# A linear map after a pooling folded into the projection before it, in a two-layer streaming encoder

## The chip, the core and the metric

The kernel runs on one core of a Trainium2 chip. A core has five engines that run side by side, each with its own instruction stream in a fixed order: TensorE (PE: matrix products and transposes; its weight loads are shown apart as PEld), VectorE (DVE), ScalarE (ACT), GpSimd (POOL) and SyncE (SP, which here only issues transfers). They work on an on-chip memory of 128 partitions; TensorE writes to a second one, PSUM, from which DVE and ACT read. The weights, the inputs and most intermediate results lie in DRAM. The metric is the device time of one execution in microseconds (us); lower is better.

## The reference

Two layers over one sequence of 2048 tokens with 1024 channels. Only layer 0's mixer matters here:

```python
def pool_mixer(h, w_in, w_group, scale, w_out):
    u, z = jnp.split(h @ w_in, 2, axis=-1)
    u = u.reshape(B, S, N_POOL_GROUPS, POOL_GROUP_DIM)      # 4 groups of 256 channels
    cs = jnp.cumsum(u, axis=1)
    ...
    for g, w in enumerate(POOL_WINDOWS):                    # 2, 4, 8, 16 frames
        ...
        means.append((cs[:, :, g] - lo) / cnt)
    pooled = jnp.stack(means, axis=2) - u
    mixed = jnp.einsum('bsgc,gcd->bsgd', pooled, w_group).reshape(B, S, D_MODEL) * scale
    return (mixed * jax.nn.silu(z)) @ w_out
```

`h` is the input after an RMS norm. For each group of channels the trailing mean over its window, minus the frame itself, is taken along the tokens; a 256 x 256 map then mixes the channels of the group. The pooling works along tokens only, with the same numbers for every channel of a group, and the map along channels only, so the two may be exchanged. After the mixer come a residual, a gated per-layer embedding, one key and value projection, and layer 1 with causal stick-breaking attention over 16 heads, a gate, an output projection and a second gated embedding.

## The kernel before

**Tiling.** The tokens are worked off in four chunks of 512 (`s`). Products run at float32 accuracy from pairs: a value is split into a high part and the rest, both in a format that TensorE reads at full rate, and each product is three matmuls (high x high, high x low, low x high) of 128 x 128 weights with 512 columns. `product` (L119) does this for two output tiles at a time over eight k-tiles: 48 matmuls. `split` (L168) makes a pair from a source: ACT casts the high part, DVE or POOL subtracts to get the low one.

**The steps of a chunk.** `steps` (L475) lists, for each chunk, 22 steps with a loader and a function that runs it. For the groups 3, 2, 1, 0 in turn there is a u step (`run_u`, L218) and a z step (`run_z`, L253); then come four output-projection steps (`run_o`, L281), four embedding steps (`run_g`, L309) and six query, key and value steps (`run_kvq`, L345). The main loop (L532) calls the loader of the next step before it runs the present one. I call a product by its step: u3 is the product of group 3's u, z2 that of group 2's z.

**The mixer.** `run_u` makes u of a group (48 matmuls), scales it by the token's norm (`ub`, L230; `rb` is that norm, broadcast), and pools it: the windowed sum is built by doubling (`us`, L236; the first and last additions on DVE, the middle ones on POOL), then `po` is the mean minus the frame (L240). In chunk 0 the first frames are corrected (L244, L245). `po` is split into the pair `pp` (L246). `run_z` makes z and SiLU(z) (L260 to L262, left in `zs`). `run_m` (L268) multiplies `pp` by the group's map (12 matmuls, the weights from `a_w_group`), then by scale and SiLU(z) (`mf`, L275), and splits the result into the pair `mp`, which `run_o` reads. `run_o` takes the k-tiles of groups 3, 2, 1, 0 in this order. `run_m` of a group stands behind the u product of the next group.

**Weights.** `load_w` (L85) loads raw weights from DRAM into the pool `wraw` (three buffers) and splits them into the pool `wpair` (twelve buffers), the input projection's with the norm's gain multiplied in (ACT at L107, DVE at L108). The split input-projection weights are stored to DRAM (`wi`, L112), and chunks 1 to 3 load them from there (L96), with no conversion. Loads and stores are issued in one queue, SP's; an issue that waits holds up those behind it. The pool `io` (ten buffers) holds the inputs and other raw tiles, `act` (18 buffers) the pairs.

**Kept weights.** `keep` (L499) loads a piece of layer 1's weights, splits it and stores it for the attention stage. The main loop calls one or two of these a step from step 8 of a chunk on.

**What sets the order.** The program's text gives a priority, and a scheduler then orders each engine's instructions ahead of time, so that a load or a split may stand well ahead of its place in the text; `tc.keep_in_program_order` takes an instruction out of this. Buffers come from pools: a new tile takes one that is free, or waits for the last reader of one. PSUM has six buffers for products (`dense`) and two for transposes (`turned`).

**Layer 1** runs in a second part (from L545 on) and is not touched. Its attention does, among others, matmuls of 128 x 128 weights with 128 to 512 columns on the diagonal blocks (L598, L599) and transposes (L623).

Of the kernel before, what the change touches and what calls it, by code (L numbers as in the profile page):

```python
# [34 lines left out]
def trunk_kernel(ctx, tc, x, p, a_norm, a_w_in, a_w_group, a_scale, a_w_out, kv_norm, w_kv,  # L35
# [46 lines left out]
    state = {"w": 0, "first": True}  # L82
    split_once = {}

    def load_w(pools, src, kts, c0, n, gain=None, kept=None):  # L85
# [6 lines left out]
        for k0 in range(0, kts, kk):  # L92
# [5 lines left out]
            raw = wraw.tile([P, kk, n], F32, tag="wraw", name="wraw")  # L98
# [20 lines left out]
    def product(pss_, units, acts, c0s, order=None):  # L119

        order = order or range(len(acts))
        for kt in order:
            for ps, c0 in zip(pss_, c0s):
                T.matmul(ps, wst(units, kt, 0, c0), acts[kt][:, 0], start=(kt == order[0]), stop=False)  # L124
                T.matmul(ps, wst(units, kt, 0, c0), acts[kt][:, 1], start=False, stop=False)  # L125
                T.matmul(ps, wst(units, kt, 1, c0), acts[kt][:, 0], start=False, stop=(kt == order[-1]))  # L126

# [7 lines left out]
    with ExitStack() as st:  # L135
# [36 lines left out]
        chunk = [{"zs": {}, "pooled": {}, "m": {}} for _ in range(NSUB)]  # L172
# [45 lines left out]
        def run_u(s, g, wu, wg=None):  # L218
            ck, win = chunk[s], WIN[g]
            pss2 = [dense(), dense()]  # L220
            product(pss2, wu, ck["x"], (0, P))
# [3 lines left out]
            pooled = []  # L225
            for k in range(2):
# [19 lines left out]
                pp = pair("pp")  # L246
                split(pp, po, V)
                pooled.append(pp)
            ck["pooled"][g] = pooled
            if wg is not None:  # L250
                run_m(s, g + 1, wg)

        def run_z(s, g, wz, wg=None):  # L253
            ck = chunk[s]
            pss2 = [dense(), dense()]
            product(pss2, wz, ck["x"], (0, P))
            zs = []
            for k in range(2):
                zr, sg = tmp("zr"), tmp("sg")
                V.tensor_tensor(out=zr, in0=pss2[k], in1=ck["rb"], op=ALU.mult)  # L260
                A.activation(out=sg, in_=zr, func=AF.Sigmoid)
                G.tensor_tensor(out=zr, in0=zr, in1=sg, op=ALU.mult)  # L262
                zs.append(zr)
            ck["zs"][g] = zs
            if wg is not None:
                run_m(s, g, wg)

        def run_m(s, g, wg):  # L268
            ck = chunk[s]
            pss2 = [dense(), dense()]  # L270
            product(pss2, wg, ck["pooled"].pop(g), (0, P))
            for k in range(2):
                o = 2 * g + k
                mf = tmp("mf")
# [599 lines left out]
```

## Time and profile before

| | |
|---|---|
| Median of 3 runs | 2869.15 us (2866.77 to 2869.49) |
| The profiled execution: its time | 2867.54 us |
| its span in the profile | 2865.7 us |
| Chunk 0: first input product to first output product | 15.02 to 132.54 us |
| Chunk 1: the same | 383.89 to 482.30 us |
| Attention's first matmul | 1416.2 us |
| DMA over the span | 576 MB, 201 GB/s |

The page of the profile gives each engine's busy time and share of the span. Its groups of instructions show the line, engine, operation, output <- input, shape and count, then busy time and mean duration, then how long the engine was idle just before them and what ended that. A timeline row gives start, duration, engine, line, operation and tiles; the bracket at its end is the idle time before it and what released it. Matmuls overlap in the pipeline, so the distance between two starts, not the duration, is what one occupies. DMA shares are means over 16 DMA engines.

### The profile page before, as it was taken

To read this page: it belongs to the slowest core of one execution; us is meant where nothing else is said; L and a number is where in the kernel's file an instruction comes from. 1 tells how busy PE (TensorE), PEld (TensorE's weight loads), DVE (VectorE), ACT (ScalarE), POOL (GpSimd) and SP (SyncE) were. 2 spreads that over 40 slices of the span, in tenths; PEclk is the share of its full clock that TensorE was granted. 3 is DMA by queue.
4 is the path that set the end of the run, shared out by engine and by line. 5 is a ranking of instruction groups with operands and counts; after the bars stand their busy time and mean duration, and the time that the engine had idled before them with its cause. 6 is when DMAs were issued, how large, how long until landed. Compare 5 with 4: busy or idle time off the path is not lost. (4 is left out here: it accounts for less than half of the span.)

```text
span 2865.7 us, 40527 instructions
## 1 busy us (share of the span) xinstructions
PE 2763.3 (96%) x13667; PEld 2273.2 (79%) x13667; DVE 1893.8 (66%) x2581; ACT 1405.6 (49%) x2765; POOL 956.2 (33%) x965
## 2 busy tenths in 40 slices
PE   8899999999999999999899999999999999999999
PEld 6688788888888888888777888787877778878877
DVE  5645535455355543555299989999999988886642
ACT  4444523355234542345255555656566655554431
POOL 3464347542474425743212121221111122213220
PEclk9999999999999999999999999999999999999999
DMA  7756696467955678446657565555555556667765
GB/s 265 257 162 216 220 305 208 143 205 250 306 160 169 223 243 287 136 153 207 212 188 229 163 216 170 159 164 177 165 161 161 163 176 193 186 188 243 251 207 158
DMA packets 335139, 576.43 MB, mean 201 GB/s; under 512 B 32782, under 2 KB 161838, under 8 KB 334932
## 3 DMA queue, kind: packets, MB, share of 16 engines
q1 hardware_dynamic: 327944, 564.34, 61.2%
q10 hardware_dynamic: 6988, 9.50, 1.1%
q8 instruction: 108, 1.77, 0.3%
q14 instruction: 99, 0.81, 0.1%
HBM read 433.16 MB, written 132.19 MB: 197 GB/s over the span
## 5 line engine op out<-in xcount | busy, mean ns | idle before, releaser
L353 PE MATMUL psd<-wpair,x 128*128 128x512 f32 x2304 | 544.8, 393 | 0.0
L602 ACT ACTIVATE kap<-psl 128x512 f32<-128x512 f32 (+3 forms) x640 | 340.3, 533 | 407.6 <-PE psl L599 398.3
L609 DVE TENSOR_TENSOR_SCAN pp<-kap,pp,zeros 128x512 f32<-128x512 f32 x384 | 512.2, 1338 | 23.3 <-ACT kap L602 21.2
L353 PEld LDWEIGHTS psd<-wpair,x 128*128 128x128 f32 x2304 | 428.8, 188 | 86.4
L623 PE MATMUL psa<-ident,pp 128*128 128x128 f32 x2176 | 348.7, 275 | 42.7 <-DVE at L627 37.9
L627 DVE TENSOR_TENSOR at<-psa,at 128x512 fp32r<-128x512 f32 (+3 forms) x640 | 373.5, 586 | 14.8 <-ACT at L626 13.8
L623 PEld LDWEIGHTS psa<-ident,pp 128*128 128x128 f32 x2176 | 263.5, 141 | 127.0 <-DVE at L627 71.2
L626 ACT CAST at<-psa 128x512 fp32r<-128x512 f32 (+3 forms) x640 | 331.3, 519 | 51.7 <-PE psa L623 48.5
L604 POOL TENSOR_SCALAR_AFFINE_SELECT kap<-kap 128x128 f32<-128x128 f32 x256 | 88.0, 345 | 633.1 <-ACT kap L602 597.9
L609 DVE TENSOR_TENSOR_SCAN pp<-kap,zeros 128x128 f32<-128x128 f32 (+3 forms) x256 | 214.2, 838 | 93.7 <-POOL kap L604 92.4
L598 PE MATMUL psl<-kk,qa 128*128 128x512 f32 (+3 forms) x640 | 235.0, 367 | 7.0 <-ACT vr L390 5.2
L635 PE MATMUL pso<-at,vv 128*128 128x512 f32 (+3 forms) x640 | 235.2, 367 | 0.8 <-ACT at L626 0.7
L599 PE MATMUL psl<-kk,qb 128*128 128x512 f32 (+3 forms) x640 | 235.1, 367 | 0.0
L636 PE MATMUL pso<-at,vv 128*128 128x512 f32 (+3 forms) x640 | 234.1, 366 | 0.0
L126 PE MATMUL psd<-xp,wpair 128*128 128x512 f32 x512 | 201.2, 393 | 4.3 <-DVE wpair L108 4.2
L124 PE MATMUL psd<-xp,wpair 128*128 128x512 f32 x512 | 201.0, 393 | 3.6 <-ACT xp L169 2.4
L108 DVE SCALAR_TENSOR_TENSOR wpair<-wraw,gains,wpair 128x512 fp32r<-128x512 f32 x192 | 149.5, 790 | 82.1 <-ACT wpair L107 81.8
L125 PE MATMUL psd<-xp,wpair 128*128 128x512 f32 x512 | 200.7, 392 | 0.0
L107 ACT ACTIVATE wpair<-wraw,gains 128x512 fp32r<-128x512 f32 x192 | 136.8, 720 | 121.0 <-DMA wraw<-in_w_kv_dram 65.9
L103 POOL TENSOR_TENSOR wpair<-wraw,wpair 128x512 fp32r<-128x512 f32 x107 | 147.7, 1388 | 78.5 <-ACT wpair L101 58.8
L101 ACT CAST wpair<-wraw 128x512 fp32r<-128x512 f32 x160 | 96.1, 619 | 124.1 <-DMA wraw<-in_a_w_out_dram 51.5
L598 PEld LDWEIGHTS psl<-kk,qa 128*128 128x128 f32 x640 | 120.9, 189 | 28.7 <-ACT vr L390 5.7
(204 smaller groups left out, 5553.4 us busy)
## 6 DMA issues: line engine op xcount, KB each, us to landing
wpair<-wi SPq DMA_DIRECT2D x96, 512.0 KB
kk<-kd SPq DMA_DIRECT2D x320, 128.0 KB
vv<-vd SPq DMA_DIRECT2D x160, 256.0 KB
wraw<-in_w_kv_dram SPq DMA_DIRECT2D x128, 256.0 KB
wpair<-wzd SPq DMA_DIRECT2D x64, 512.0 KB
wpair<-wod SPq DMA_DIRECT2D x64, 512.0 KB
wpair<-wgd SPq DMA_DIRECT2D x64, 512.0 KB
wi<-wpair SPq DMA_DIRECT2D x32, 512.0 KB
```

Of the source, the lines that this page charges most:

```text
L124: T.matmul(ps, wst(units, kt, 0, c0), acts[kt][:, 0], start=(kt == order[0]), stop=False)
L126: T.matmul(ps, wst(units, kt, 1, c0), acts[kt][:, 0], start=False, stop=(kt == order[-1]))
L353: T.matmul(pss2[i], ck["x2"][kt][:, xh, tk], wst(ws, kt, wh, 0, W5), start=(kt == 0 and xh == 0 and wh == 0), stop=(kt == KT - 1 and wh == 1))
L598: T.matmul(ps[:, :w], qa[:, qs], kk[:, :w], start=True, stop=False)
L599: T.matmul(ps[:, :w], qb[:, qs], kk[:, :w], start=False, stop=True)
L602: A.activation(out=kp[:, r0:], in_=ps[:, :w], func=AF.Sigmoid, scale=-1.0)
L609: V.tensor_tensor_scan(out=pp[:, r0:][:, ::-1], data0=kp[:, r0:][:, ::-1], data1=zeros.to_broadcast([P, w]), initial=1.0 if st["diag"] els ...
L623: T.transpose(pt[:, j * P : (j + 1) * P], pp[:, r0 + kt * P : r0 + (kt + 1) * P], ident)
L626: A.copy(out=at[:, 0, cs], in_=pt[:, cs])
L627: V.tensor_tensor(out=at[:, 1, cs], in0=pt[:, cs], in1=f(at[:, 0, cs]), op=ALU.subtract)
L635: T.matmul(po[:, cs], vv[:, kt, :], at[:, 0, cs], start=(st["diag"] and kt == 0), stop=False)
L636: T.matmul(po[:, cs], vv[:, kt, :], at[:, 1, cs], start=False, stop=(st["last"] and kt == 3))
```

## The change

The group map goes from the pooled activations to the weights. In chunk 0, for each group, the weights of u (1024 x 256) are multiplied by the group's 256 x 256 map once, with the norm's gain, on TensorE; the product is split into a pair and stored as the input-projection weight. u made with it is already mapped, so that `run_m` is gone in all chunks, and `po` is multiplied by scale and SiLU(z) at once and split into `mp`.

- z now comes ahead of u in each group, since u's step needs SiLU(z).
- `load_fold` loads a group's raw u weights (into pairs of the pool `act`) and its map. `fold` transposes the raw weights in blocks of 128 x 128 (`across`: 16 transposes and four splits into `wt` for a group), then multiplies (`mapped`: four times 12 matmuls with 256 columns), and evicts with the gain on ACT and DVE.
- `product` takes a list of pieces of work, `beside`, and calls one after each k-tile: in chunk 0's z products the four `across` and then the four `mapped`.
- While `state["deep"]` is set (the loaders called in steps 0 to 6), raw weights go into `io`'s ten buffers instead of `wraw`'s three.
- `keep`'s load keeps its place in program order.

```diff
     def load_w(pools, src, kts, c0, n, gain=None, kept=None):
...
-            raw = wraw.tile([P, kk, n], F32, tag="wraw", name="wraw")
+            if state["deep"]:
+                raw = io.tile([P, kk, n], F32, tag="io", name="wraw")
+            else:
+                raw = wraw.tile([P, kk, n], F32, tag="wraw", name="wraw")
...
-    def product(pss_, units, acts, c0s, order=None):
+    def product(pss_, units, acts, c0s, order=None, beside=()):
+        beside = iter(beside)
...
+            next(beside, None)
+        for _ in beside:
+            pass
...
+        def load_fold(g):
+            raws = []
+            wg = load_w(wp, a_w_group[0, g], 2, 0, 256)[0]
+            for p0 in range(0, KT, 4):
+                raw = f(pair("uraw"))
+                raws += [raw[:, e].rearrange("q (k n) -> q k n", k=2) for e in range(2)]
+                def load(raw=raw, p0=p0):
+                    nc.sync.dma_start(
+                        out=raw.rearrange("q e (k n) -> q (e k) n", k=2),
+                        in_=a_w_in[0].rearrange("(k q) n -> q k n", q=P)[:, p0 : p0 + 4, g * 256 : (g + 1) * 256])
+                if g == 3:
+                    late.append(load)
+                else:
+                    load()
+            return raws, wg
+
+        def fold(g, raws, wg):
+            units = chunk[0].setdefault("wu", {})[g] = []
+            wts = []
+            def across(i):
+                pt = turned()
+                for ct in range(2):
+                    for e in range(2):
+                        T.transpose(pt[:, 2 * ct + e, :], raws[i][:, e, ct * P : (ct + 1) * P], ident)
+                wt = pair("wt")
+                split(wt, pt.rearrange("q j t -> q (j t)"), V)
+                wts.append(wt)
+            def mapped(i):
+                ps = dense()
+                for e in range(2):
+                    n = 0
+                    for ct in range(2):
+                        ks = slice((2 * ct + e) * P, (2 * ct + e + 1) * P)
+                        for wh, gh in ((0, 0), (0, 1), (1, 0)):
+                            T.matmul(ps[:, e * 256 : (e + 1) * 256], wts[i][:, wh, ks], wg[:, gh, ct, :],
+                                     start=(n == 0), stop=(n == 5))
+                            n += 1
+                pr = wpair.tile([P, 2, 2, 256], F32R, tag="wpair", name="wpair")
+                for e in range(2):
+                    ga = g_a[:, 2 * i + e : 2 * i + e + 1]
+                    A.activation(out=pr[:, 0, e], in_=ps[:, e * 256 : (e + 1) * 256], func=AF.Identity, scale=ga)
+                    V.scalar_tensor_tensor(out=pr[:, 1, e], in0=ps[:, e * 256 : (e + 1) * 256], scalar=ga,
+                                           in1=f(pr[:, 0, e]), op0=ALU.mult, op1=ALU.subtract)
+                units.append(pr)
+                d = split_once["wi", g * 256, 2 * i] = dram.tile([P, 2, 2, 256], F32, name=f"wu_{g}_{i}")
+                nc.sync.dma_start(out=d, in_=f(pr))
+            for i in range(4):
+                across(i)
+                yield
+            for i in range(4):
+                mapped(i)
+                yield
+
+        def run_z(s, g, wz):
...
+            product(pss2, wz, ck["x"], (0, P), beside=fold(g, *ck["fold"].pop(g)) if not s else ())
             settle()
...
+        def run_u(s, g, wu):
+            product(pss2, wu or ck["wu"].pop(g), ck["x"], (0, P))
...
-                pp = pair("pp")
-                split(pp, po, V)
-                pooled.append(pp)
...
-        def run_m(s, g, wg):
-            product(pss2, wg, ck["pooled"].pop(g), (0, P))
...
+                V.scalar_tensor_tensor(out=po, in0=po, scalar=g_s[:, o : o + 1], in1=ck["zs"][g][k],
                                        op0=ALU.mult, op1=ALU.mult)
                 pr = pair("mp")
-                split(pr, mf, G)
+                split(pr, po, G if g else V)
...
+                def load(g=g, s=s, z=0):
+                    if not s and z and g < 3:
+                        chunk[0]["fold"][g] = load_fold(g)
+                    if not s and not z:
+                        return (None,)
+                    return (load_w(wp, a_w_in[0], KT, z * D + g * 256, 256, g_a, "wi"),)
+                steps.append((lambda load=load: load(z=1), lambda *w, s=s, g=g: run_z(s, g, *w)))
                 steps.append((load, lambda *w, s=s, g=g: run_u(s, g, *w)))
...
-            nc.sync.dma_start(out=raw, in_=src.rearrange("(k q) n -> q k n", q=P)[:, k0 : k0 + kts, o * P : (o + 1) * P])
+            tc.keep_in_program_order(nc.sync.dma_start(
+                out=raw, in_=src.rearrange("(k q) n -> q k n", q=P)[:, k0 : k0 + kts, o * P : (o + 1) * P]))
...
         ready = steps[0][0]()
+        chunk[0]["fold"][3] = load_fold(3)
         state["first"] = False
         for _ in first:
             pass
+        settle()
...
         for i, (_, run) in enumerate(steps):
+            state["deep"] = i < 7
             after = steps[i + 1][0]() if i + 1 < len(steps) else None
```

60 lines of the change are left out of this document (18 added, 42 removed).

## The prediction

> **What bounds the kernel now.** I read the busy shares first, then the stretches of the first stage, then the timeline of TensorE for the spacing of its matmuls.
>
> ```profile
> PE 2763.3 (96%) x13667; PEld 2273.2 (79%) x13667; DVE 1893.8 (66%) x2581; ACT 1405.6 (49%) x2765; POOL 956.2 (33%) x965
> ...
> 75.00:100.00 25.00, 22.64 (x92) 18.00 (x92) 15.76 (x31) 7.97 (x18) 8.99 (x10) 0.93 0.81 284
> 125.00:150.00 25.00, 20.16 (x71) 14.80 (x70) 15.64 (x19) 12.75 (x25) 21.07 (x19) 0.86 0.60 194
> 383.89:481.80 97.91, 97.91 (x435) 81.06 (x434) 46.21 (x66) 30.69 (x59) 59.44 (x57) 1.00 0.80 274
> 775.00:800.00 25.00, 25.00 (x112) 20.68 (x111) 9.37 (x13) 5.95 (x12) 11.85 (x13) 1.00 0.94 321
> ```
>
> The columns of the last four rows are the stretch, its length, the busy time of PE, PEld, DVE, ACT and POOL, the granted clock, the DMA share and GB/s. TensorE bounds the kernel. The third stretch is chunk 1's whole input stage (u, z and mapped products), busy for 97.91 of 97.91 us: there a matmul less is time less. Chunk 0 is different. It converts the raw weights, and in 75 to 100 us and 125 to 150 us PE idles, and the clock falls to 0.93 and 0.86. Its waits are these:
>
> ```profile
> L126 PE MATMUL psd<-xp,wpair 128*128 128x512 f32 x512 | 201.2, 393 | 4.3 <-DVE wpair L108 4.2
> L124 PE MATMUL psd<-xp,wpair 128*128 128x512 f32 x512 | 201.0, 393 | 3.6 <-ACT xp L169 2.4 <-ACT wpair L107 1.2
> ...
> ACT wpair L107 <- DMA wraw<-in_a_w_in_dram: 34.4, 15, 7.4
> ...
> SPq L112 <- DVE wpair L108: 51.4, 28, 5.0
> ```
>
> The conversions wait 34.4 us for raw weights, because SP's queue itself stands 51.4 us at stores that wait for a conversion, with the next loads queued behind them. PE pays 4.2 + 1.2 = 5.4 us of it directly.
>
> **The change, part by part.** *The mapped products go.* They are the matmuls that read pp:
>
> ```profile
> L125 PE MATMUL psd<-pp,wpair 128*128 128x512 f32 x64 | 26.0, 406 | 2.4 <-DVE pp L170 2.4
> L124 PE MATMUL psd<-pp,wpair 128*128 128x512 f32 x64 | 25.7, 402 | 1.4 <-ACT pp L169 1.4
> L126 PE MATMUL psd<-pp,wpair 128*128 128x512 f32 x64 | 25.6, 400 | 0.0
> ...
> L125 PE MATMUL psd<-mp,wpair 128*128 128x512 f32 x256 | 100.8, 394 | 2.8 <-POOL mp L170 2.6
> L126 PE MATMUL psd<-mp,wpair 128*128 128x512 f32 x256 | 100.4, 392 | 1.9 <-POOL wpair L103 1.9
> ...
> 1156.35 0.39 PE L124 MATMUL psd<-pp,wpair 128*128 128x512 f32 x1
> 1156.58 0.39 PE L125 MATMUL psd<-pp,wpair 128*128 128x512 f32 x1
> ```
>
> One takes 0.39 us but the next starts 0.2267 us later (12 of them fill 2.72 us), and that spacing is its price. 3 x 64 = 192 matmuls x 0.2267 = 43.5 us go: 144 of them (32.6 us) in the dense chunks 1 to 3, 48 (10.9 us) in chunk 0. With them go PE's waits for pp, 1.4 + 2.4, and at the output product behind them, 2.6 + 1.9: 8.3 us. The pooled pairs' split (32 ACT casts, 32 DVE subtractions) and 12 loads and splits of the map go too. They lay beside PE, on engines 49% and 66% busy, and count nothing.
>
> *The fold comes, in chunk 0 alone.* For each of four groups there are 16 transposes and 48 matmuls with 256 columns: 64 transposes and 192 matmuls. Attention's diagonal block shows both shapes:
>
> ```profile
> 1488.29 0.28 PE L598 MATMUL psl<-kk,qa 128*128 128x256 f32 x1
> 1488.30 0.19 PEld L599 LDWEIGHTS psl<-kk,qb 128*128 128x128 f32 x1
> 1488.41 0.28 PE L599 MATMUL psl<-kk,qb 128*128 128x256 f32 x1
> ...
> 1488.53 0.60 PE L623 MATMUL psa<-ident,pp 128*128 128x128 f32 x4
> ...
> 1488.88 0.48 PE L664 MATMUL psd<-x,wpair 128*128 128x512 f32 x1
> ...
> 1489.20 0.39 PE L666 MATMUL psd<-x,wpair 128*128 128x512 f32 x1
> ```
>
> A 256-column matmul holds PE for 0.12 us (1488.29 to 1488.41 to 1488.53): 192 x 0.12 = 23.0 us. The rows are only two in a line. The lower bound is half of 0.2267, so 21.8 us; the upper is the 0.19 us weight load as the pace of a long run of them, 36.5 us. I take 0.12, since the load of L599 starts with the matmul of L598 and runs under it. Four transposes take 0.35 us, and the matmul behind them is late by 0.32 - 0.23 = 0.09: 0.44 a block, 16 blocks, 7.0 us.
>
> A rule of the Trainium skill speaks against that ("TensorE: Matmul & The Clock Gate", Part 3, The mechanism): a weight load overlaps a running matmul only if it goes to other row groups. All loads here use the full array, so by it each would stand in line. The row at 1488.30 disagrees: that load overlaps. By the rule the time would be rival E's, by the row the forecast's.
>
> *Where the fold stands.* In the built order of the changed kernel, the first group's fold is interleaved with z3's product and has its inputs early. In z2, z1 and z0 the first mapped matmul stands behind 37, 31 and 30 matmuls of that z product and eight transposes. PE gets there 37 x 0.2267 + 0.88 = 9.3 us, 7.9 us and 7.7 us after the u product before it. What it reads (wt, the split transposes) is queued on ACT behind the casts of both mp of that u group, and on DVE behind the whole pooling chain. So the chain's length decides:
>
> ```profile
> 57.28 1.28 DVE L230 TENSOR_TENSOR ub<-psd,rbx 128x512 f32<-128x512 f32 x2
> ...
> 61.55 0.69 DVE L240 SCALAR_TENSOR_TENSOR po<-us,ub 128x512 f32<-128x512 f32 x1 [2.37 <-POOL us L236]
> ...
> 87.63 1.28 DVE L230 TENSOR_TENSOR ub<-psd,rbx 128x512 f32<-128x512 f32 x2
> 88.83 0.70 DVE L236 TENSOR_TENSOR us<-ub 128x527 f32<-128x527 f32 x1
> 90.77 0.69 DVE L240 SCALAR_TENSOR_TENSOR po<-us,ub 128x512 f32<-128x512 f32 x1 [1.24 <-POOL us L236]
> ...
> 96.89 1.26 POOL L236 TENSOR_TENSOR us<-us 128x525 f32<-128x525 f32 x1 [6.16 <-DVE po L245]
> ...
> 772.90 0.69 DVE L240 SCALAR_TENSOR_TENSOR po<-us,ub 128x512 f32<-128x512 f32 x1 [2.37 <-POOL us L236]
> ...
> 777.05 0.69 DVE L240 SCALAR_TENSOR_TENSOR po<-us,ub 128x512 f32<-128x512 f32 x1 [2.09 <-POOL us L236]
> ...
> 1101.07 0.69 DVE L236 TENSOR_TENSOR us<-us 128x513 f32<-128x513 f32 x1 [4.21 <-POOL us L236]
> ...
> 1106.68 0.69 DVE L240 SCALAR_TENSOR_TENSOR po<-us,ub 128x512 f32<-128x512 f32 x1
> ...
> L275 DVE SCALAR_TENSOR_TENSOR mf<-psd,gains,zr 128x512 f32<-128x512 f32 x32 | 23.3, 743 | 11.8 <-POOL zr L262 11.8
> ...
> L169 ACT CAST mp<-mf 128x512 fp32r<-128x512 f32 x32 | 19.4, 619 | 11.6 <-DVE mf L275 11.1
> ```
>
> Group 2 (window 8): 57.28 to 61.55 until the first tile's po, 4.3 us, and 772.90 to 777.74 for the second, 4.8: 9.1 us. Group 3 (window 16) needs the same 4.3 until its last addition and then 1101.07 to 1107.37: 10.6 us. Group 1 (window 4): 87.63 to 90.77, then po, an addition, POOL's 1.26 and po, 3.3: 6.5 us. Then follow about 0.3 of chunk 0's corrections, 0.74 for the scale and gate (as L275), 0.62 for the cast of mp and as much for wt: 2.3 us. So wt is there 12.9, 11.4 and 8.8 us after the u product. z2 waits 3.6 us, z1 3.5. z0 waits for wt's low half too (0.7 more, since the third transposes need that buffer): 1.8. With 1 us for the two small gain transposes in z3, whose loads now queue behind two 512 KB loads and four stores: 9.9 us. Bounds: nothing, if the chain overlaps the tail of the u product, and 18 us if POOL's work beside it doubles each of these waits.
>
> Behind the mapped products nothing waits: the u product takes the PSUM buffers of the first two mapped products, read long before z's own.
>
> *The buffers.* Up to ten raw weights instead of three may be in flight, and loads of z2, z1 and even the output projection stand ahead of the stores. This removes the 5.4 us. Without that cover they come back. The kept weights of layer 1 leave chunk 0's input stage, because their loads now keep program order; SP moves the same bytes later, beside output products, where DMA is 60% busy.
>
> *The output product.* Before, mp was late by one POOL subtraction; now the whole chain of group 0 stands behind u0. It reads groups 3, 2, 1 first: 36 matmuls, 8.2 us of cover. The chain without POOL's additions is ub 1.28, two additions 1.4, two po 1.4, two gates 1.5: 5.6 us, then the split 0.7 each. This fits, but in chunk 0 corrections, a weight subtraction and kept weights stand between on DVE (about 4 us more). I put back 2.4 us in chunk 0 and, for POOL working beside, 0.6 in each other chunk: 4.2 us. Bounds: 0 and 8.
>
> *The clock.* In the rows of 75 to 100 us and 125 to 150 us, where PE idles, 0.93 of 25 us is 1.75 us of clock lost, and 0.86 is two of these: 5.2 us go with the waits. I expect three new ones, in z2, z1 and at chunk 0's output product: 5.2 come.
>
> **Sum**: -43.5 - 8.3 - 5.4 - 5.2 + 23.0 + 7.0 + 9.9 + 4.2 + 5.2 = -13.1 us. The profiled execution took 2867.5 us: 2854.4. It is 1.6 under the median of the runs, 2869.15, so I say **2856 us**.
>
> **Rivals.** A, *the fold finds its inputs*: no wait in z2, z1, z0 and no half clock there, 9.9 + 3.5 less: 2842.6. For it: the folds' engines are far from full. Against it: the order puts wt last on two queues.
> B, *weight loads pace the 256-column runs* at 0.19: + 13.5, 2869.5. Against it: loads hide in the two-matmul rows; for it: nothing longer is shown.
> C, *transfers become the bound of chunks 1 to 3*, slower: 274 GB/s x 97.91 us = 26.8 MB, less 0.8 of the map, in a stage shortened to 87 us. If 274 GB/s is all that this mix gets, it takes 95 us, 8 us more in each chunk: 2880. It decides below 26.0 MB / 87 us = 299 GB/s. Against it: no product waited for wpair there, and 321 GB/s was moved elsewhere.
> D, *DVE and POOL hold each other up* in chunk 0's chains, slower:
>
> ```profile
> 816.57 2.40 DVE L236 TENSOR_TENSOR us<-ub 128x527 f32<-128x527 f32 x2
> ...
> 116.35 1.31 DVE L236 TENSOR_TENSOR us<-ub 128x527 f32<-128x527 f32 x2
> ```
>
> The same two additions take 2.40 us beside POOL's subtractions and 1.31 alone. If every chain (12.9, 11.4, 8.8, and 9.6 for group 0) grows by 2.40/1.31, that is 42.7 x 0.83 = 35 us of waits: 2891. From 19 us of them on, the kernel is slower. Against it: in chunk 0 POOL has little else to do between the additions.
> E, *weight loads don't hide*: 0.19 + 0.12 each, 192 x 0.19 = 36.5 more, 2892.5.
>
> **How the numbers follow.** Forecast 0.60 (its own range 2846 to 2866), A 0.16, B 0.06, C 0.05, D 0.10, E 0.03, which has a row against it and none for it. Faster by over 0.2% means under 2863.4; runs of this kernel differ by 0.1%, so 0.2% is what can be told from no change. Faster: A and 0.56 of the forecast, 0.72. Within 0.2%: B and the forecast's upper end, 0.10. Slower: C, D, E, 0.18. The range is 2840 to 2872: it leaves out C, D and E (0.18) and a little below A.
>
> **What would show it.** Right: chunks 1 to 3's input stages at 87 us, dense; 12 mapped matmuls in 1.44 us; in chunk 0 waits of PE for ACT's wt in z2 and z1, 3 to 4 us each; raw weights never late. Wrong: mapped matmuls 0.19 apart (B) or 0.31 (E); PE waiting for wpair from DRAM (C); waits of over 6 us in each z product (D) or none (A).

## The result, and the profile after

The changed kernel takes **2891.88 us** (median of 6 runs, 2890.1 to 2899.43), the kernel before, beside it on the same chip, 2867.44 us (2863.35 to 2869.49): a ratio of 1.0091, with a 95% interval of 1.008 to 1.0102. It is slower by 24 us; forecast were 2856 us, and 2840 to 2872 us as the range. The profiled execution took 2899.43 us, the slowest of the six, so its stages add up to some 7 us more than the median shows.

The page of the changed kernel, busy times first, then the group that lost most:

```profile
PE 2773.1 (96%) x13731; PEld 2285.4 (79%) x13731; DVE 1881.2 (65%) x2569; ACT 1387.6 (48%) x2737; POOL 927.6 (32%) x949
...
L406 PE MATMUL psd<-wpair,x 128*128 128x512 f32 x2304 | 559.9, 400 | 17.1 <-ACT x L177 16.9
```

The same group, with its old line number, in the groups of the kernel before:

```profile
L353 PE MATMUL psd<-wpair,x 128*128 128x512 f32 x2304 | 544.8, 393 | 0.0
```

These are the k, v and q products, which the change does not touch. They never waited before; now they wait 16.9 us for a cast of x, and one takes 400 ns where it took 393, because the clock drops behind the waits. Cut at the first matmul of each kind, the stages of the two profiled executions compare so (us; the last two columns are experiments told below):

| stage | before | changed | loads free | pieces placed |
|---|---|---|---|---|
| chunk 0, input | 117.5 | 146.7 | 146.2 | 125.1 |
| chunks 1 to 3, input | 297.8 | 262.5 | 262.5 | 262.7 |
| output, four | 186.0 | 188.1 | 196.7 | 182.5 |
| gate, four | 218.1 | 218.1 | 218.1 | 218.1 |
| k, v, q, four | 581.7 | 613.6 | 580.4 | 590.8 |
| attention to the end | 1449.5 | 1453.4 | 1450.5 | 1455.1 |

The fold pays what it promised in chunks 1 to 3 (35.3 us). Chunk 0 costs 29.2 us, of which the forecast had about 21. The 31.9 us in the k, v and q stages were not in it at all.

The stretches of the changed kernel (length, busy PE, PEld, DVE, ACT, POOL, clock, DMA share, GB/s), chunk 0's input stage, its k, v, q stage, chunk 1's input stage, and the k, v, q stages of chunks 1 and 3:

```profile
15.26:162.00 146.74, 133.94 (x670) 114.17 (x671) 78.50 (x134) 55.52 (x115) 43.33 (x45) 0.94 0.50 178
...
262.56:419.22 156.66, 149.29 (x682) 121.84 (x681) 76.61 (x117) 78.07 (x141) 53.69 (x49) 0.96 0.65 217
419.22:506.72 87.50, 87.50 (x389) 72.46 (x388) 35.01 (x49) 21.54 (x40) 51.00 (x50) 1.00 0.74 255
...
610.79:768.46 157.67, 150.50 (x682) 122.81 (x681) 75.72 (x115) 79.38 (x143) 53.50 (x49) 0.95 0.64 217
...
1300.58:1444.28 143.70, 139.96 (x650) 114.95 (x648) 67.49 (x98) 65.66 (x108) 50.36 (x46) 1.00 0.66 218
```

The stage of chunk 0 and its like in chunk 1 take 157 us at a clock of 0.95 to 0.96; chunk 3's takes 143.7 us at 1.00. Before, all four took 144.2 to 147.6. What holds the cast of x is seen where PE first waits, at the turn from the gate products to the first q product of chunk 0 (timeline of the changed kernel, picked from five engines):

```profile
264.57 0.42 SPq L553 DMA_DIRECT2D kraw<-in_b_w_out_dram  x1
...
269.82 0.62 ACT L177 CAST kpair<-kraw 128x512 fp32r<-128x512 f32 x1 [4.14 <-DMA kraw<-in_b_w_out_dram]
...
270.52 1.27 POOL L178 TENSOR_TENSOR kpair<-kraw,kpair 128x512 fp32r<-128x512 f32 x1 [5.11 <-ACT kpair L177]
271.75 1.26 POOL L381 TENSOR_TENSOR sg<-sg,x 128x512 f32<-128x512 f32 x1
...
273.04 0.69 DVE L383 TENSOR_TENSOR tx<-sg,x 128x512 f32<-128x512 f32 x1 [5.82 <-POOL sg L381]
273.77 0.62 ACT L177 CAST x<-tx 128x512 fp32r<-128x512 f32 x1 [2.70 <-DVE tx L383]
...
274.44 3.23 PE L406 MATMUL psd<-wpair,x 128*128 128x512 f32 x6 [3.56 <-ACT x L177]
279.00 3.23 PE L406 MATMUL psd<-wpair,x 128*128 128x512 f32 x6 [1.33 <-ACT x L177]
```

Read it downwards. The raw tile of a kept weight (kraw) is asked for at 264.57. ACT reaches its cast and stands there 4.14 us until the tile lands. POOL reaches the subtraction of the same piece and stands 5.11 us, with the sum for the gate (sg) queued behind it. DVE then waits 5.82 us for that sum, ACT casts x, and PE, which had everything else, has waited 3.56 us and soon 1.33 more. In the kernel before no kept weight stands in this place. The wait is not all: in the 25 us behind it the clock is 0.76, which is 6 us more.

```profile
275.00:300.00 25.00, 23.67 (x86) 18.63 (x86) 9.48 (x17) 10.42 (x21) 10.57 (x11) 0.76 0.57 198
```

Where the kept weights' 56 pieces stand, counted by ACT's conversions in each kind of stage (all four chunks): before 39 in input, 2 in output, none in gate and 15 in k, v, q stages; now 8, 14, 12 and 22.

In chunk 0's input stage the forecast waits are there (timeline of the changed kernel):

```profile
34.49 1.59 PE L274 MATMUL psd<-wpair,wt 128*128 128x256 f32 x12
35.91 0.40 PE L129 MATMUL psd<-xp,wpair 128*128 128x512 f32 x1
...
68.13 0.62 ACT L177 CAST mp<-po 128x512 fp32r<-128x512 f32 x1 [4.07 <-DVE po L335]
68.66 1.06 ACT L177 CAST wt<-pst 128x512 fp32r<-128x512 f32 x2
...
69.29 0.80 PE L274 MATMUL psd<-wpair,wt 128*128 128x256 f32 x2 [4.09 <-ACT wt L177]
```

Twelve mapped matmuls fill 35.91 - 34.49 = 1.42 us, 0.118 each. In z2 PE waits 4.09 us for wt, which ACT casts only behind both casts of mp.

### The profile page after: what moved, and what is told of

Its sections match the earlier page's. It is cut to its first block, busy times and chain, and to the rows that moved or that the text cites. A ratio compares the mean times of both kernels' runs of the same rounds, so it can differ in the third digit from the quotient of the medians.

```text
span 2897.6 us, 40532 instructions
## 1 busy us (share of the span) xinstructions
PE 2773.1 (96%) x13731; PEld 2285.4 (79%) x13731; DVE 1881.2 (65%) x2569; ACT 1387.6 (48%) x2737; POOL 927.6 (32%) x949
## 5 line engine op out<-in xcount | busy, mean ns | idle before, releaser
L406 PE MATMUL psd<-wpair,x 128*128 128x512 f32 x2304 | 559.9, 400 | 17.1 <-ACT x L177 16.9
L406 PEld LDWEIGHTS psd<-wpair,x 128*128 128x128 f32 x2304 | 435.2, 191 | 111.5 <-ACT x L177 20.6
L106 POOL TENSOR_TENSOR wpair<-wraw,wpair 128x512 fp32r<-128x512 f32 x99 | 137.5, 1395 | 118.5 <-ACT wpair L104 97.3
L691 PEld LDWEIGHTS pso<-at,vv 128*128 128x128 f32 x640 | 120.8, 189 | 26.4 <-ACT at L682 1.6
```

The source lines that it names most:

```text
L406: T.matmul(pss2[i], ck["x2"][kt][:, xh, tk], wst(ws, kt, wh, 0, W5), start=(kt == 0 and xh == 0 and wh == 0), stop=(kt == KT - 1 and wh == 1))
L691: T.matmul(po[:, cs], vv[:, kt, :], at[:, 0, cs], start=(st["diag"] and kt == 0), stop=False)
```

## The experiments

Two theories stood first. **K**: the loss comes with the kept weights' loads in program order, by the conversions that now stand among the gate and q products. **F**: it comes with the fold and the start of chunk 0.

**Undo the order alone, do the order alone.** In the changed kernel, and the other way round in the kernel before:

```diff
-            tc.keep_in_program_order(nc.sync.dma_start(out=raw, ...))
+            nc.sync.dma_start(out=raw, ...)
```

> The changed kernel, only that the load of a kept weight of layer 1 is again free to be moved ahead of its place in the program. Theory K (the loss is in the k, v and q products of chunks 0 to 2, where a kept weight lands after its conversion's turn, and the conversion stands ahead of x's casts): the three stages fall from 155.6-157.7 us to about 145 with no wait of PE for an x cast, and the output stages from 49.5 to about 46; some 35 us go. Part of that comes back in chunk 0, where these conversions will stand beside the fold: I expect 2862 to 2872 us. Rival F (the fold and the start of chunk 0 make the loss): the three stages stay at 155 and the time at 2888 to 2895 us.

> The kernel before, with one call added: the loads of the kept weights keep program order. Theory K: the same waits as in the changed kernel, in the same places: kvq stages of chunks 0 to 2 at 154 to 158 us (145 now), so + 25 to + 32 us in these; chunk 0's input stage gets up to 5 us shorter, since the kept weights' transfers leave it: 2887 to 2897 us. Rival F: within 3 us of 2867 us.

Without the order: 2873.16 us, ratio 1.0024 (1.0014 to 1.0034). With the order alone in the kernel before: 2903.61 us, ratio 1.013 (1.0115 to 1.0145). Both lie above what theory K gave, by 1 and by 7 us. The group of the k, v and q products in the one and the other:

```profile
L406 PE MATMUL psd<-wpair,x 128*128 128x512 f32 x2304 | 544.9, 393 | 0.0
```

```profile
L353 PE MATMUL psd<-wpair,x 128*128 128x512 f32 x2304 | 561.6, 400 | 19.9 <-ACT x L169 19.6 <-DVE x L170 0.2
...
L169 ACT CAST kpair<-kraw 128x512 fp32r<-128x512 f32 (+1 forms) x40 | 23.0, 576 | 111.9 <-DMA kraw<-in_b_w_out_dram 44.8 <-DMA kraw<-in_ple_gate_w_dram 42.6 <-DMA kraw<-in_ple_w_dram 20.4
```

The waits go with the call and come with it, fold or no fold: F is not what makes the loss in these stages. It is not out of the account, though: without the order the changed kernel is still 8 us slower than the kernel before, where 13 us faster were forecast. The order costs the kernel before 38 us and the changed kernel 19: freeing the loads takes 33 us out of the k, v and q stages, but puts 9 into the output stages. Of the 37 us between forecast and result, the order makes 19; most of the rest stands in chunk 0's input stage and, with free loads, in the output stages.

**Load one step ahead; hold the conversion too; load by another queue.** Each kept weight is loaded, still in program order, one step before it is converted. Then its cast on ACT also keeps its place, behind the casts of its step. Then the load goes through ACT's queue. In the edit, `keep` stops between load and conversion, and `keep_on` loads the next piece and converts the one loaded before.

```diff
-                kept.pop(0)()
+                keep_on()
...
-                split(pr, raw, G)
+                tc.keep_in_program_order(A.copy(out=pr[:, 0], in_=raw))
+                G.tensor_tensor(out=pr[:, 1], in0=raw, in1=f(pr[:, 0]), op=ALU.subtract)
...
-            tc.keep_in_program_order(nc.sync.dma_start(
+            tc.keep_in_program_order(nc.scalar.dma_start(
```

> The changed kernel, with each kept weight loaded one step ahead of its conversion, still in program order. Theory K (a load that lands late): kvq stages at 144 to 147 us without waits for x casts, chunk 0's input stage as it is (147 us): 2856 to 2864 us. Rival W (the load is not what is late; the conversions' own work on ACT, POOL and DVE at that place holds x's casts up): kvq stages stay at 152 us and above, the time at 2882 us and above.

> The changed kernel, with each kept weight loaded one step ahead as in the run before, and its conversion on ACT now held at its place in the program too, behind the casts of its step. Theory L (loading ahead alone did nothing because the planner moved the conversion forward to right behind its load; what holds x's casts up is a conversion that stands in front of them and waits for its transfer): k, v and q stages of chunks 0 to 2 fall to 144 to 147 us without waits for x casts, 2857 to 2868 us. Rival W (the conversions' own work and transfers at that place): the stages stay at 152 us or more, 2882 us or more.

> The run before with the kept weights' loads ahead and their conversions held (2883.9 us), only that the loads are issued by ACT's queue and not by SP's. Theory Q (a load that keeps its place on SP is a wall in SP's queue: the raw weights of the next products stand behind it and behind the stores of its step, land late, and their conversions hold x's casts up): with SP's queue free the k, v and q stages of chunks 0 to 2 fall from 152.6-157.2 to 144 to 147 us, and the time to 2855 to 2866 us. Rival W (the kept weights' own conversions and transfers beside these products cost it, wherever the load is queued): the stages stay at 151 us or more, the time at 2878 us or more.

2897.02 us (1.0108, 1.0083 to 1.0133), 2883.94 us (1.007, 1.0055 to 1.0085) and 2896.22 us (1.011, 1.0093 to 1.0126). In all three the theory under test missed; the k, v and q stages of chunks 0 to 2 stay at 151 to 157 us, and stages and times are where rival W put them (the pieces cost something at that place, whichever way they are loaded). In the first the scheduler moved the cast forward to its load again (its timeline):

```profile
260.60 0.43 SPq L553 DMA_DIRECT2D kraw<-in_ple_gate_w_dram  x1
...
264.05 0.62 ACT L177 CAST kpair<-kraw 128x512 fp32r<-128x512 f32 x1 [2.34 <-DMA kraw<-in_ple_gate_w_dram]
```

In the second no kept weight waits any more (3.3 us over all 40 casts), yet x does. So a conversion that waits for its own load is not the whole of it. In the third the k, v and q stages come to 153, 151 and 151 us with SP's queue free of these loads, and the gate stages get 3 to 8 us longer with waits for p's tiles.

**Free loads, held conversions.**

> The changed kernel with the kept weights' loads free to move on SP, but their conversions on ACT held at their place behind the casts of their step. Theory Q: no wall on SP, so k, v and q stages at 144 to 147 us; no conversion ahead of a cast that PE waits for, so the output stages fall from the 47 to 52 us of the run with free loads and free conversions to 44 to 46 us; chunk 0's input stage stays at 146 us. Together 2855 to 2863 us. Rival W: the conversions at that place cost what they cost in the changed kernel: stages at 151 us or more, 2878 us or more.

2876.33 us, ratio 1.004 (1.0025 to 1.0056): output stages of chunks 1 to 3 at 44.3, as expected, k, v and q stages at 148, 155, 155 and 149, not as expected. Its groups, then its timeline at the same turn as above:

```profile
L406 PE MATMUL psd<-wpair,x 128*128 128x512 f32 x2304 | 555.7, 398 | 12.1 <-ACT x L177 10.4 <-DVE x L178 1.7
...
L556 ACT CAST kpair<-kraw 128x512 fp32r<-128x512 f32 (+1 forms) x40 | 22.5, 567 | 1.1 <-DMA kraw<-in_b_w_out_dram 1.0
```

```profile
262.75 0.32 SPq L564 DMA_DIRECT2D wod<-kpair  x1
263.17 1.73 SPq L102 DMA_DIRECT2D wraw<-in_b_w_in_dram  x3
...
267.15 0.73 ACT L110 ACTIVATE wpair<-wraw,gains 128x512 fp32r<-128x512 f32 x1 [4.72 <-DMA wraw<-in_b_w_in_dram]
267.78 0.60 ACT L177 CAST x<-tx 128x512 fp32r<-128x512 f32 x1
...
273.09 0.51 PE L406 MATMUL psd<-wpair,x 128*128 128x512 f32 x1 [1.23 <-ACT x L177]
```

Now the piece's store (wod) is what stands in the way. SP issues three raw q weights only behind it, ACT waits 4.72 us for one of these, and x's cast stands behind. PE waits only 1.23 us for it here; in chunks 1 and 2, where the same rows come again, 3.1 and 4.1 us. With the load out of the way, another part of the same piece takes its place. That spoke for the place as the cause, as rival W had it: theory **P**.

**Change the place.** First the pieces of chunk 0 and chunk 3 are exchanged; then, with the loads still in program order, all are moved out of the output, gate and first q steps.

```diff
-            if step >= 8 and (s + 1 < NSUB or step < 16):
-                kept.pop(0)()
-                if s + 1 < NSUB and step in (8, 12):
-                    kept.pop(0)()
+            for _ in range(2 if s and step < 7 else 1 if step >= 17 and s + 1 < NSUB else 0):
+                if kept:
+                    kept.pop(0)()
```

> The changed kernel, with the kept weights' pieces of chunk 0 and chunk 3 exchanged: chunk 0 gets the eight that chunk 3 had, chunk 3 the sixteen of chunk 0. Theory P (a kept weight's piece costs by the place where it stands: conversion, store and load among the gate products and the first q product delay x's casts there): the k, v and q stage of chunk 0 falls from 156.7 to 143.5 to 147 us, that of chunk 3 rises from 143.7 to 153 us or more, the time stays within 4 us of 2892. Rival (chunk 0's loss comes from the fold's late end or from its stores, chunk 3's freedom from having no next chunk to load): chunk 0's stage stays above 152 us and chunk 3's below 147 us.

> The changed kernel, with the loads still in program order, but the pieces at another place in the program: two behind each u and z product of chunks 1 to 3 but the last, the others behind q1 and the k and v products; none among the output and gate products. Theory P: all four k, v and q stages at 143 to 147 us, output stages at 44 to 46, and chunk 1 to 3's input stages stay at 87.5 us, since DVE, ACT and POOL have room there: 2852 to 2862 us. Rival (the pieces only move their price): the input stages rise to 90 us and more each and the time stays at 2870 us or above.

The exchange: 2908.45 us (1.0144, 1.0124 to 1.0163), above what either theory gave. Chunk 3's stage rises from 143.7 to 159.6 us, but not by waits for x, which are 1.3 us there. Behind its last product, at the edge to attention, PE now waits for ACT's last v tile and then for keys (timeline of this run):

```profile
1456.77 1.08 PE L753 MATMUL psar<-ident,r2all 128*128 128x128 f32 x4 [5.31 <-ACT vr L443]
1464.58 0.44 PE L654 MATMUL psl<-kk,qa 128*128 128x128 f32 x1 [6.72 <-DMA kk<-kd]
```

From the last k, v or q matmul to attention's first it takes 13.5 us, in the changed kernel 3.9: 9.6 of the 15.9 us. So the pieces cost chunk 3 too, but mostly by another way than theory P says. Chunk 0's falls to 154.0 only, not to 145, with 4.9 us of waits for ACT's cast of x as before: the eight pieces that cost nothing in chunk 3 cost something in chunk 0. Why is open. The move: 2923.7 us (1.0199, 1.0178 to 1.0221). Where the pieces left, the loss is gone, k, v and q stages of chunks 0 to 2 at 144.9, 144.9 and 147.2 us. But the input stages of chunks 1 to 3 take 96, 104 and 100 us, and the output stages 56 to 57: as the rival said, in this order the pieces only move their price. Chunk 1's input stage in this run (stretch and SP's timeline), then the same stage in the run with free loads, which has 11 pieces in it:

```profile
405.04:501.27 96.23, 88.26 (x389) 72.12 (x388) 36.19 (x54) 23.96 (x51) 54.24 (x53) 0.99 0.84 288
```

```profile
442.20 0.43 SPq L553 DMA_DIRECT2D kraw<-in_b_w_out_dram  x1
442.68 0.84 SPq L553 DMA_DIRECT2D kraw<-in_ple_gate_w_dram  x1
443.62 1.11 SPq L96 DMA_DIRECT2D wpair<-wi  x2
449.04 0.32 SPq L564 DMA_DIRECT2D wod<-kpair  x1
450.30 0.32 SPq L564 DMA_DIRECT2D wgd<-kpair  x1
450.67 0.45 SPq L553 DMA_DIRECT2D kraw<-in_b_w_in_dram  x1
```

```profile
408.67:496.18 87.51, 87.51 (x390) 72.46 (x389) 35.38 (x54) 24.84 (x49) 53.92 (x52) 1.00 0.83 296
```

In order, SP goes from a piece's load to its store and stands there 4.3 us (443.62 + 1.11 to 449.04), with the next weights behind it; PE idles 8 us in the stage, 3.4 of them put down to such a weight. Free, the same stage moves 296 GB/s, over 25 us of it (435 to 460) 401 GB/s, and PE is busy for all of it. So 288 GB/s is not a bound of the transfers; the stand in the queue accounts for the 3.4 us, and for the rest of the 8 the trace names no releaser.

**The smaller terms of chunk 0.** The raw weights in three buffers as before; wt made (`across`) beside the u product of the group ahead; the map and the raw u weights of group 3 loaded behind x's casts.

```diff
-            state["deep"] = i < 7
+            state["deep"] = False
...
-            product(pss2, wu or ck["wu"].pop(g), ck["x"], (0, P))
+            product(pss2, wu or ck["wu"].pop(g), ck["x"], (0, P), beside=beside())
...
-        chunk[0]["fold"][3] = load_fold(3)
         state["first"] = False
...
-        settle()
         for _ in prep(0):
             pass
+        chunk[0]["fold"][3] = load_fold(3)
+        settle()
```

> The changed kernel, with the raw weights of the first stage in the three buffers of before. If the free buffers remove what the prediction credits them with, PE's waits for the conversions of raw weights come back, 5.4 us and one or two half clocks of 1.75 us: 2897 to 2902 us. Rival: with the fold there are fewer raw weights in the way (the u weights' raw tiles have buffers of their own), and three buffers do: 2890 to 2894 us.

> The changed kernel, with the transposes and splits of the next group's raw weights (wt) put into the u product ahead, before that group's pooling chain. Theory Z (in chunk 0 the mapped products wait because wt is queued behind the pooling chain): PE's waits for wt, 8.15 + 2.61 us, and the two half-clock windows of 6.8 us behind them (3.4 us lost each) go; chunk 0's input stage falls from 146.7 to 128 to 134 us and the time by 12 to 18 us, to 2874 to 2880 us. Rival (the wait moves: the pooling chain, now behind the splits, makes mp or z late instead): the input stage and output stage of chunk 0 together change by less than 6 us.

> The changed kernel, with the map of group 3 loaded and converted behind x's transposes and casts. Theory S (the map's conversion stands ahead of the casts of x at the start, PE waits 2.04 us there and stays at half clock to 27.6 us): chunk 0's input stage falls by 5 to 8 us, to 139 to 142 us, and the time to 2884 to 2887 us. Rival: the start is bound by x's transfers, and the map then comes too late for z3's mapped products: no gain, 2891 us or more.

Three buffers: 2893.34 us (1.0103, 1.0086 to 1.012), no difference from the changed kernel's 1.0091, and no wait of PE for a raw weight's conversion: the free buffers are worth nothing here. wt early: **2876.99 us** (1.0042, 1.0028 to 1.0057), chunk 0's input stage 128.3 us at a clock of 0.99 instead of 146.7 at 0.94: 15 us, as theory Z said. The late map: the stage falls to 139.9 us as expected, but the time is 2895.86 us (1.0107, 1.0091 to 1.0122), no gain that shows, as its rival had it. How far the stage's fall is the map's is taken up below.

**Together.** Free loads, wt early, the late map; the same with held conversions; the same with ACT's queue; the pieces moved in order, with both repairs, conversions free and held.

> Three edits together on the changed kernel: the kept weights' loads free to move, wt made in the u product ahead, the map of group 3 behind x's casts. If the losses are separate and add (kept weights 19 us as measured, wt 12 to 18, start 5 to 8): 2848 to 2858 us, faster than the kernel before (2865). Rival: with free loads the kept weights' conversions come back into chunk 0 and take the place of what was cleared there: chunk 0's input stage stays above 135 us and the time at 2862 us or more.

> The run with free loads and held conversions, and with it wt made in the u product ahead and the map of group 3 behind x's casts. If the parts add (chunk 0's input stage at 128 us, the output stages at 44 to 46, k, v and q stages at 145): 2836 to 2846 us, 20 to 30 us under the kernel before. Rival: the parts share a cover, and it stays at the 2857 us of the three edits with free conversions.

> The run with the kept weights' loads on ACT's queue, and with it wt made in the u product ahead and the map of group 3 behind x's casts. By theory Q 2836 to 2848 us. Rival W: 2858 us or more, since the k, v and q stages stay at 151 us or more.

> That place for the kept weights, and with it wt made in the u product ahead and the map of group 3 behind x's casts. If the parts add: chunk 0's input stage at 125 to 128 us, the rest as in the run before: 2828 to 2842 us, 23 to 37 us under the kernel before. Rival: 2850 us or more.

> The same three edits, and the conversions of the kept weights on ACT held at their place too. If a conversion that the planner moves forward waits for its load in the input stages and holds mp up, this is 2 to 8 us faster than the run without; if nothing there is on the path, the same within 2 us.

In that order 2857.19 us (0.9969, 0.9959 to 0.9978), 2861.4 us (0.998, 0.9971 to 0.999), 2876.09 us (1.0036, 1.0024 to 1.0048), 2908.84 us (1.015, 1.0135 to 1.0165) and 2906.65 us (1.0143, 1.0127 to 1.0159). The repairs of chunk 0 hold in all five (its input stage is at 124 to 129 us); the first is in its range, 9 us faster than the kernel before. The second, third and fourth miss theirs and bring along what their handling of the kept weights cost alone; the fifth is 2.2 us under the fourth, too little to tell its two outcomes apart. The first still loses in the output stages (49.2 to 52.1 us, against 44.3 in the second). A try at that gives the raw weights of the output products the shared buffers:

```diff
-            state["deep"] = i < 7
+            state["deep"] = i < 7 or 7 <= i % STEPS < 11
```

> The three edits with free loads and free conversions (2857 us), and the raw weights of the output products in the ten shared buffers in every chunk instead of the three of their own. In that run the output stages took 49.2 to 52.1 us where 44.3 are dense, because the chain of u0's pooling on DVE stands behind conversions of output weights that wait for their loads, and the loads wait for one of three buffers. If so, the output stages fall to 44.5 to 47 us each and the time by 10 to 18 us, to 2840 to 2848 us. Rival: the kept weights take the buffers, or the chain itself is the limit: within 5 us of 2857 us.

2868.29 us (1.0003, 0.9994 to 1.0012), output stages 52 to 56 us: worse. Its timeline shows what stands in front of u0's chain now, a kept weight that waits for its load:

```profile
489.10 1.28 ACT L587 ACTIVATE kpair<-kraw,gains 128x128 fp32r<-128x128 f32 x4 [7.49 <-DMA kraw<-in_b_w_in_dram]
...
489.54 1.23 DVE L588 SCALAR_TENSOR_TENSOR kpair<-kraw,gains,kpair 128x128 fp32r<-128x128 f32 x4 [7.13 <-ACT kpair L587]
490.68 1.28 DVE L346 TENSOR_TENSOR ub<-psd,rbx 128x512 f32<-128x512 f32 x2
```

**The pieces placed.** Loads free, conversions held, and the place chosen.

```diff
+            for _ in range(1 if s and step < 4 else 1 if 8 <= step < 11 else 2 if step >= 17 and s + 1 < NSUB else
+                           1 if step == 11 and s in (1, 2) else 0):
+                kept.pop(0)()
```

> wt made in the u product ahead, the map of group 3 behind x's casts, the kept weights' loads free on SP, their conversions on ACT held at their place, and that place chosen: one behind each of the first four products of chunks 1 to 3, one behind each of the first three output products, two behind q1 and each k and v product; none among the last output product, the gate products and the first q product. If place and waiting are what costs, all stages are near their dense time: chunk 0's input stage 125 us, output stages 44.3 to 49, k, v and q stages 143 to 147 us: 2828 to 2843 us, faster than the kernel before by 23 to 37 us. Rival (whatever place they get, the pieces cost 8 us or more a chunk): 2852 us or more.

**2849.06 us** (2847.74 to 2853.02), ratio 0.9937 (0.9923 to 0.995): the fastest version, 17 us under the kernel before, if 6 us above the range expected of it and 3 under its rival's. From the second version of those together (2861.4 us) it differs by the place alone, so the place is worth 12 us. PE waits for no cast of x (its groups):

```profile
L433 PE MATMUL psd<-wpair,x 128*128 128x512 f32 x2304 | 547.1, 394 | 0.0
...
L583 ACT CAST kpair<-kraw 128x512 fp32r<-128x512 f32 (+1 forms) x40 | 22.3, 572 | 15.7 <-DMA vs<-vr 14.6 <-DMA wgd<-kpair 0.5 <-DMA wraw<-in_w_kv_dram 0.3
```

The k, v and q stages of chunks 0 to 2 still take 149 us: there the pieces stand two to a step beside the k and v products, and PE waits 2.7 to 3.6 us for hl. The output stages are at 44.3 to 48.4.

## Why the prediction was wrong

**The step that failed.** "The kept weights of layer 1 leave chunk 0's input stage, because their loads now keep program order; SP moves the same bytes later, beside output products, where DMA is 60% busy." It counted bytes and found room for them. A kept weight is also a cast on ACT, a subtraction on POOL or DVE and a store on SP, and in the rows above each stands in front of other work of its engine. Priced at nothing, this step measured 31.9 us in the k, v and q stages of the profiled execution, and 19 us net in the times with and without the order. Its working left out what it asked for elsewhere: which instruction stands behind the moved one, on each engine, and who waits for that. That the order is the cause of this loss is shown from both sides, by taking it out and by adding it alone. That the place matters is shown by the pieces leaving the stage and the loss with them, and by the 12 us of the placed version. Which part of a piece hurts most is not settled: each that was relieved was followed by another.

**The clock.** Each new wait was priced with 1.75 us of half clock. Behind the first wait in chunk 0's q product it was 6 us, and in that stage the clock of 0.96 is 0.04 x 156.66 = 6.3 us beside 7.3 us of waits. In chunk 0's input stage, where the forecast had 3.5 us for z2 and z1, the clock is at 0.50 in three stretches, at or just behind the waits in z2, z1 and z0:

```profile
68.52:75.35 6.83, 6.06 (x27) 5.97 (x28) 2.70 (x5) 2.85 (x6) 1.28 (x1) 0.50 0.00 0
102.66:109.49 6.83, 5.12 (x22) 4.82 (x23) 3.19 (x5) 2.76 (x5) 1.28 (x1) 0.50 0.06 15
140.21:143.62 3.41, 3.41 (x14) 3.02 (x14) 1.72 (x4) 1.44 (x3) 0.00 (x0) 0.50 0.03 5
```

Half of these 17.1 us is 8.5. The size was off by a factor of two to three here; that it is not a fixed price is shown in the last section.

**Chunk 0's input stage.** Its terms lead to about 139 us (117.5 - 10.9 - 2.4 - 5.4 - 3.5 + 30.0 + 9.9 + 3.5); it took 146.7. (Of the 5.2 us of clock that the forecast took off, 1.7 lies at 135.2 to 138.6 us, in the output stage.) Without waits and their clock the terms give 125.3 us, and the stage of the placed version, which has next to none of either, takes 125.1:

```profile
14.85:139.96 125.11, 124.71 (x670) 106.27 (x671) 77.36 (x134) 54.87 (x115) 43.68 (x45) 1.00 0.64 227
```

So the work was priced right, and the waits and the clock were not. Between the two stages PE's busy time grows by 133.94 - 124.71 = 9.2 us at the same work, by the lower clock, where 3.5 were forecast; its waits are 12.8 us, where 9.9 were. The waits for wt were mis-sized by little: 8.15 + 2.61 = 10.8 us against 3.6 + 3.5 + 1.8 = 8.9, in the places and for the reason given. The rest of the waits is at the start, for which the forecast had only "the two small gain transposes", at 1 us (timeline of the changed kernel, ACT and PE):

```profile
19.20 0.62 ACT L104 CAST wpair<-wraw 128x512 fp32r<-128x512 f32 x1 [1.05 <-DMA wraw<-in_a_w_group_dram]
...
20.35 1.05 ACT L177 CAST xp<-pst 128x512 fp32r<-128x512 f32 x2
...
21.69 1.11 PE L217 MATMUL pst<-ident,xin 128*128 128x128 f32 x4 [2.04 <-DVE xp L178]
```

The cast of group 3's map (L104) waits for its load in front of x's casts, and PE waits 2.04 us behind them. With it moved, this wait is gone and the stage was 6.8 us shorter, but these are not the map's alone: with the loads one step ahead the map stands where it stood, PE waits 1.98 us there, and the stage is 6.2 us shorter too.

**What held.** Chunks 1 to 3's input stages: forecast 87 us and dense, measured 87.50 with PE busy for 87.50; against the 98.39 us of the kernel before with the order alone, that is 32.6 us in the three, as forecast. Waits at the output products: 4.2 us forecast, 6.1 measured (1.4, 3.0, 0 and 1.7). Mapped matmuls: 0.12 us forecast, 0.118 measured, so rivals B and E fall. The rule that the forecast cited for E ("TensorE: Matmul & The Clock Gate", Part 3, The mechanism, in the Trainium skill) does not describe these loads: by it each would stand in line, and the 1.42 us for twelve leave no room for that. (The same section of the Trainium skill also lets a load run ahead into a background weight buffer; whether these loads do, no run here tells.) Rival C falls too: no wait for weights from DRAM, and 296 GB/s in the same stage of another run. Rival D named a time close to the measured one for a cause that did not occur; the waits in z2 and z1 were 4.1 us each, not over 6. The raw weights are never late, as forecast, but not because of the free buffers: with three the same holds. That the u weights no longer pass through these buffers may be why, or that the kept weights have left the stage: the order alone takes it from 117.5 to 112.4 us in the kernel before. Neither was tried apart: with the kept weights back in the stage (loads free) there were ten buffers, and still no such wait.

## What to carry to other kernels

When a change pins, frees or moves one instruction, follow everything that belongs to its tile to its new place (load, conversion, store) and name, for each engine's queue there, what stands behind it; bytes that fit are no proof that the queue does. Work that is off the critical path wants a place where the next product waits least for the engines that it uses; here the place alone was worth 12 us, with the order of the loads left free. A wait in a dense product can cost twice itself, by the clock.

## What was not expected of the hardware

The clock's loss behind the same waits varies. Chunk 0's input stage of the changed kernel has 12.8 us of waits that the trace puts down to a releaser, and a clock of 0.94; with the loads one step ahead these are 12.7 us, at the same places, and the stage takes 140.56 us, at 0.98 (two stretches at half clock, then the whole stage):

```profile
67.63:71.04 3.41, 3.41 (x19) 3.41 (x17) 1.57 (x3) 1.17 (x2) 0.00 (x0) 0.50 0.00 0
101.77:105.18 3.41, 3.41 (x17) 3.31 (x16) 1.38 (x2) 1.52 (x3) 0.00 (x0) 0.50 0.32 101
15.22:155.78 140.56, 127.89 (x671) 108.76 (x671) 78.14 (x134) 55.21 (x115) 43.24 (x45) 0.98 0.52 186
```

Where the changed kernel has half clock for 6.83, 6.83 and 3.41 us, this run has it for 3.41 and 3.41 us. That is 6 us between two executions with equal waits, about what a small experiment tries to measure. The Trainium skill ("TensorE: Matmul & The Clock Gate", Part 1, What's actually happening) says that the window by which the gate judges activity runs freely, so that the moment at which the clock changes depends on where in it the first matmul lands. For waits inside a stage that would make the loss depend on where they fall; the two stages agree with that, and no run here tests it. A stage's length is therefore read with its clock beside it, and a version that removes the waits (125.1 us at 1.00, against 146.7 with 12.8 us of waits) gains more than their sum.
